# Low parts of two output weights in an attention and convolution kernel: subtracted by GpSimd behind the scaling of the probabilities, or by VectorE behind the row maximum

## The chip, the cores and the metric

The kernel runs on one core of one Trainium2 chip. A core has five engines that run their own instruction rows and wait for each other by semaphores: TensorE (PE in the profile, with its weight loads as PEld), VectorE (DVE), ScalarE (ACT), GpSimd (POOL) and SyncE (SP, which here only issues DMAs). The metric is the device time of one execution in microseconds (us), the median of the runs.

## The reference, cut to what matters

Two layers work on 1024 latent tokens of width 1024, with 256 context tokens. The first is attention with a window of 128 on each side, 16 query heads on 4 key heads, a learned sink in the softmax and a gate; the second is a gated convolution of width 31. Each ends in an output projection with a weight of 2048 x 1024:

```python
p_ctx, p_win = sink_softmax(sink_l, s_ctx, s_win)
o = einsum('bhgqc,bchd->bqhgd', p_ctx, vc) + einsum('bhgqk,bkhd->bqhgd', p_win, vw)
y = (o * silu(z)) @ attn_w_out            # first layer
...
y = (u * silu(z)) @ conv_w_out            # second layer
x = x + gate * y
```

All is float32. The kernel gets near this with TensorE's rounded float32 by splitting each operand into a rounded high part and the rest, the low part, and adding three products: high by high, high by low, low by high.

## The kernel before, in words

Everything is tiled in 128 partitions. SBUF is held as 45 pages of 1024 words (`pg`, line 113) and 6 half pages of 528 words (`hp`, line 114), which go round in a queue: a page that is freed is given out again, and its new writer waits for its last reader.

The program has three stages. First come the norms and modulation of the first layer. Then attention (lines 1083 to 1127) goes through 16 heads of 8 query blocks, 128 steps. Last come the first output projection, the convolution layer and the second output projection. TensorE's row is kept in the order of the program (`pin("P")`, line 1064); the rows of the other engines are set by a scheduler that simulates the kernel, within the dependencies, so that an edit can move instructions which it does not name.

One attention step does this. TensorE computes the scores of the next block into a PSUM tile `pss` (`scores`, line 938). VectorE adds mask and sink and takes the row maximum (`p_page<-pss,mask_page,nsink`, a custom instruction, line 966, with a read of its accumulator into `sc`). ScalarE takes the exponential in place (`p_page,sc<-p_page,sc`, line 968), VectorE the reciprocal of the row sum (`sc<-sc`, line 969), GpSimd scales the probabilities by it (`p_page<-p_page,sc`, line 970). Meanwhile TensorE runs 12 matmuls of the projections of the next head (`psg<-hh_page,whi_page` and the like, `fill(FILL)`, line 1105). Then it transposes the scaled probabilities of the block before (`pss<-ident,p_page`, `transposes`, line 973). ScalarE rounds the transposed block into `pthi`, VectorE subtracts that from it into `ptlo` (lines 991 and 992). Every fourth step TensorE multiplies `pthi` and `ptlo` by the values (`pso<-pthi,kvc_page`, `pv`, line 994). The scores and the transposes share two PSUM tiles, so that the scores of a step wait for the `ptlo` or the maximum that last read the tile.

Beside the steps run these jobs. The weights of the projections are loaded (`wraw_page`), rounded by ScalarE (`whi_page`), and GpSimd subtracts (`wlo_page<-wraw_page,whi_page`, 128 x 1024). The queries of the next head are rotated: ScalarE copies them, a DMA swaps halves, GpSimd multiplies by the sines (`rope_half<-rope_half,sin_page`), VectorE adds, ScalarE rounds (`qh_page`), and GpSimd subtracts (`ql_page<-rope_half,qh_page`). VectorE also sums the modulation of the second layer (`mask_page<-wsum_raw,cs,mask_page` and the same with `dww_raw`, `ada_rest`, line 566).

One more job is `low_parts` (line 613): 32 pieces of the two output weights, two rows of 512 words each, are loaded into a page (`low_page`), ScalarE rounds each half into a half page (`lhi_half`, line 622), the difference replaces the half (`low_page<-low_page,lhi_half`, 128 x 512, line 623), and SP stores the page to DRAM (`wolA<-low_page`, `wolC<-low_page`, line 627), from where the projections read it later. That is 64 subtractions, done by VectorE. The helper `after` (line 561) adds an ordering without a semaphore: VectorE's subtraction stands behind the last row maximum (`anchor_max`).

Of the kernel before, what the change touches and what calls it, by code (L numbers as in the profile page):

```python
# [12 lines left out]
ALU = mybir.AluOpType  # L13
# [80 lines left out]
def backbone_kernel(  # L94
# [8 lines left out]
    V, A, G, PE, SY = (InOrder(tc, e) for e in (nc.vector, nc.scalar, nc.gpsimd, nc.tensor, nc.sync))  # L103
# [18 lines left out]
    def ps_s():  # L122
        return ps.tile([P, 1024], F32, tag="s", name=nm("pss"), bufs=2)
# [21 lines left out]
    def small(shape, dt=F32, name="sm", bufs=2):  # L145
        return cpool.tile(shape, dt, tag=f"{name}", name=nm(name), bufs=bufs)

    def act(out, in_, func, **kw):
        return A.activation(out=out, in_=in_, func=func, **kw)

    def tt(eng, out, a, b, op):
        return eng.tensor_tensor(out=out, in0=a, in1=b, op=op)
# [4 lines left out]
    def split_lo(eng, lo, full, hi):  # L157
        return tt(eng, lo, full, hi.bitcast(F32), ALU.subtract)
# [333 lines left out]
    for pr in range(NPR):  # L492
        a, b = 2 * pr, 2 * pr + 1
# [51 lines left out]
    mask = mask_pg[:, 0:768]  # L545
# [10 lines left out]
               for t, n in (("dww", NJ * TAPS), ("wsum", NJ * 16))]  # L556

    anchor = []
    anchor_max = []

    def after(ins, anchor=anchor):
        if anchor:
            tc.add_manual_dep(ins.ins, anchor[0].ins.name, mybir.DependencyInfo(
                mybir.DependencyClass.NoSync, mybir.DependencyReason.DATA), reason="behind the softmax")
# [44 lines left out]
    def pair_rows(ap, m, kk):  # L609

        return ap[kk * 256:kk * 256 + 256, m * 512:m * 512 + 512].rearrange("(a p) n -> p a n", p=P)

    def low_parts():

        items = [(pair_rows(w, m, kk), d[m, kk]) for w, d in ((Wo, wolA), (Wp, wolC)) for m in range(2) for kk in range(NK)]
        for src, dst in items:
            raw = pg.alloc(F32, [2, 512], "low")
            SY.dma_start(out=raw, in_=src)
            yield "open"
            for b in range(2):  # L620
                hi = hp.alloc(F32R, None, "lhi")
                act(hi[:, 0:512], raw[:, b], AF.Copy)
                after(split_lo(V, raw[:, b], raw[:, b], hi[:, 0:512]), anchor_max)
                hp.free(hi)
                if b == 0:
                    yield "open"
            SY.dma_start(out=dst, in_=raw)
            pg.free(raw)
            yield "shut"
# [308 lines left out]
    def scores(h, qb):  # L938
        g = h // 4
        q = qt[h]  # L940
        kk = kvt[g]
        c = kk[2]
        k0, k1 = max(qb - 1, 0), min(qb + 1, TB - 1)
        nw = (k1 - k0 + 1) * P
        s = ps_s()
        w0 = 512 - nw
        qsl = slice(qb * P, qb * P + P)
        ksl = slice(k0 * P, k0 * P + nw)
        for n, (a, b) in enumerate(((0, 0), (0, 1), (1, 0))):
            PE.matmul(s[:, w0:512], q[a][:, qsl], kk[b][:, ksl], start=n == 0, stop=n == 2)  # L950
            PE.matmul(s[:, 512:768], q[a][:, qsl], c[:, b], start=n == 0, stop=n == 2)
        p = pg.alloc(F32, [1024], "p")
        sc8 = small([P, 3], name="sc", bufs=6)
        nmx, l0, ri = (sc8[:, i:i + 1] for i in range(3))
        w = nw + CT

        act(p[:, w:w + 1], nsink[:, h:h + 1], AF.Copy)
        sc = dict(scale=-SCALE, scalar=nsink[:, h:h + 1], op0=ALU.add, op1=ALU.min, accum_out=nmx)
        if qb == TB - 1:
            least = V.tensor_tensor_reduce(  # L960
                out=p[:, 0:w].rearrange("p (a b) -> p a b", a=2),
                in0=s[:, w0:768].rearrange("p (a b) -> p a b", a=2),
                in1=mask.rearrange("p (a b) -> p a b", a=2)[:, :, 0:256],
                **sc)
        else:
            least = V.tensor_tensor_reduce(out=p[:, 0:w], in0=s[:, w0:768], in1=mask[:, 640 - w:640], **sc)
        anchor_max[:] = [least]
        act(p[:, 0:w + 1], p[:, 0:w + 1], AF.Exp, bias=nmx, scale=-1.0, accum_out=l0)
        V.reciprocal(ri, l0)
        G.tensor_scalar(out=p[:, 0:w], in0=p[:, 0:w], scalar1=ri, scalar2=1.0, op0=ALU.mult, op1=ALU.mult)  # L970
        ptile[(h, qb)] = p

    def transposes(h, qb):
# [73 lines left out]
    for kt in range(KT):  # L1047
        x_mm(kt, 1, acc1, range(3))
        if kt + 2 < KT:
            x_tile(turn(xs1, kt + 2, lambda: ps_o(kt % 2)), kt + 2, 1, G if kt % 2 and kt > 1 else V)  # L1050
        if kt > 2 and ropes0:
            ropes0.popleft()()
        if kt == 3:
            ctx0("v", 2)
        if kt >= 2 and tails:
            tails.pop(0)()
        if kt == 0:
            wsA.load()
        if kt == 5:
            pg.free(*xs1)  # L1060
            wsA.split()
        if kt == KT - 1:
            scores(0, 0)
# [6 lines left out]
    while len(tails) > 1:  # L1070
        tails.pop(0)()
    steps = [(h, qb) for h in range(NH) for qb in range(TB)]
    lows = low_parts()
    lstate = ["shut"]
    pvq = deque()
# [7 lines left out]
    for i, (h, qb) in enumerate(steps):  # L1083
# [18 lines left out]
        if nxt and not regroup:  # L1102
            scores(*nxt)
# [4 lines left out]
        if regroup:  # L1108
            g = nxt[0] // 4
            old = kvt[g - 1]  # L1110
            run(job(("k", g)))
            transposes(h, qb)
            run(job(("v", g)))
            pv(h, 1)
            pg.free(*old)
            scores(*nxt)
            vlate.pop(g)()
            continue
# [576 lines left out]
```

## Time and profile before

| what | value |
|---|---|
| runs of the kernel before | 1777.82, 1778.02, 1778.15 us; median 1778.02 |
| the profiled execution | 1782.36 us, its span 1780.1 us |
| TensorE busy | 1722.9 us, 97% of the span |
| VectorE, ScalarE, GpSimd busy | 1203.3, 885.6, 780.4 us |
| mean granted TensorE clock | 0.991 |
| HBM read and written | 188.70 MB and 41.69 MB |

A row of the timeline gives start, duration, engine, line, operation, what is written from what, shapes and, in brackets, how long the engine idled before it and what released it. All instructions go through one helper (line 88), so they are told apart by the names of their tiles. In the answers by tile, least, median and longest durations are in ns. Times in the windows and the timeline are us from the span's start. The profiled execution is 4.34 us longer than the median of the runs.

### The profile page before, as it was taken

How to read it: one execution, taken by the hardware profiler on the slowest of the kernel's cores; microseconds unless marked ns; L12 is line 12 of the kernel's file. 1: busy time of each engine (PE TensorE's matmuls, PEld its weight loads, DVE VectorE, ACT ScalarE, POOL GpSimd, SP SyncE). 2: the span in 40 equal slices, each digit the busy share in tenths (PEclk: the TensorE clock that was granted, in tenths of full speed). 3: DMA queues.
4: the chain of work that ended last, by engine and by line, in shares of the span. 5: the costliest groups of instructions: out<-in, count | busy, mean ns of one | idle time of the engine just before them, and what ended most of it. 6: DMA issues, size and time to landing. Idle time of an engine off the chain costs nothing. (4 is left out here: it accounts for less than half of the span.)

```text
span 1780.1 us, 23728 instructions
## 1 busy us (share of the span) xinstructions
PE 1722.9 (97%) x8383; PEld 1419.1 (80%) x8383; DVE 1203.3 (68%) x2165; ACT 885.6 (50%) x1540; POOL 780.4 (44%) x610
## 2 busy tenths in 40 slices
PE   5999999999999999999999999999999999999997
PEld 2788888788887888788888887888888888787886
DVE  6766774667555664666314269999999999866823
ACT  6555543455344453444433445654656565456730
POOL 0244343333423343432100247998988789120300
PEclk8999999999999999999999999999999999999999
DMA  9334443444234443336776733111121212377881
GB/s 311 102 81 139 143 127 93 125 147 145 80 116 131 142 150 93 114 100 206 256 248 241 260 94 102 29 48 36 36 83 36 73 46 71 120 245 237 311 281 48
DMA packets 195322, 242.43 MB, mean 136 GB/s; under 512 B 11798, under 2 KB 126790, under 8 KB 195204
## 3 DMA queue, kind: packets, MB, share of 16 engines
q1 hardware_dynamic: 188516, 230.10, 39.8%
q10 hardware_dynamic: 6688, 10.83, 2.6%
q8 instruction: 66, 1.08, 0.3%
q14 instruction: 52, 0.43, 0.1%
HBM read 188.70 MB, written 41.69 MB: 129 GB/s over the span
## 5 line engine op out<-in xcount | busy, mean ns | idle before, releaser
L88 POOL TENSOR_TENSOR odd_half<-odd_half,prod_half 128x513 f32<-128x513 f32 (+2 forms) x252 | 317.9, 1269 | 20.8 <-ACT prod_half L88 7.3
L88 POOL TENSOR_TENSOR wlo_page<-wraw_page,whi_page 128x1024 fp32r<-128x1024 f32 x71 | 173.8, 2449 | 153.0 <-ACT whi_page L88 115.6
L88 POOL TENSOR_SCALAR p_page<-p_page,sc 128x640 f32<-128x640 f32 (+1 forms) x128 | 104.2, 815 | 307.7 <-DVE sc L88 280.2
L88 PE MATMUL psg<-hh_page,whi_page 128*128 128x512 f32 x600 | 237.6, 396 | 0.0
L88 PE MATMUL psg<-hh_page,wlo_page 128*128 128x512 f32 x600 | 236.3, 394 | 0.0
L88 PE MATMUL psg<-hl_page,whi_page 128*128 128x512 f32 x600 | 236.0, 393 | 0.0
L88 ACT ACTIVATE prod_half<-ubuf,dww 128x513 f32<-128x513 f32 (+2 forms) x252 | 165.0, 674 | 108.6 <-POOL odd_half L88 104.4
L88 PE MATMUL psg<-h2l_page,whi_page 128*128 128x512 f32 x456 | 180.6, 396 | 1.8 <-DVE h2l_page L88 1.8
L88 PE MATMUL psg<-h2h_page,whi_page 128*128 128x512 f32 x456 | 181.5, 398 | 0.0
L88 PE MATMUL psg<-h2h_page,wlo_page 128*128 128x512 f32 x456 | 180.1, 395 | 0.0
L88 DVE SCALAR_TENSOR_TENSOR pss<-ubuf,wsum,pss 128x512 f32<-128x512 f32 (+3 forms) x270 | 172.3, 671 | 0.3
L88 DVE SCALAR_TENSOR_TENSOR pss<-ubuf,dww,pss 128x512 f32<-128x512 f32 (+3 forms) x270 | 172.1, 671 | 0.3
L88 ACT ACTIVATE p_page<-p_page,sc 128x641 f32<-128x641 f32 (+1 forms) x128 | 102.9, 804 | 91.8 <-DVE sc L88 87.3
L88 ACT ACTIVATE pthi<-pss 128x640 fp32r<-128x640 f32 (+1 forms) x144 | 88.7, 616 | 104.7 <-PE pss L88 98.0
L88 DVE TENSOR_TENSOR ptlo<-pss,pthi 128x640 fp32r<-128x640 f32 (+1 forms) x144 | 103.1, 716 | 45.7 <-ACT pthi L88 45.3
L88 PEld LDWEIGHTS psg<-hh_page,wlo_page 128*128 128x128 f32 x600 | 112.8, 188 | 26.2
L88 ACT ACTIVATE whi_page<-wraw_page 128x1024 fp32r<-128x1024 f32 x88 | 92.8, 1054 | 73.9 <-PE psg L88 22.3
L88 PEld LDWEIGHTS psg<-hl_page,whi_page 128*128 128x128 f32 x600 | 112.9, 188 | 20.1
L88 PEld LDWEIGHTS psg<-hh_page,whi_page 128*128 128x128 f32 x600 | 112.8, 188 | 20.0
L88 PE MATMUL pso<-h2l_page,whi_page 128*128 128x512 f32 x312 | 122.9, 394 | 0.0
L88 PE MATMUL pso<-h2h_page,wlo_page 128*128 128x512 f32 x312 | 122.8, 393 | 0.0
L88 PE MATMUL pso<-h2h_page,whi_page 128*128 128x512 f32 x312 | 122.7, 393 | 0.0
(240 smaller groups left out, 4026.8 us busy)
## 6 DMA issues: line engine op xcount, KB each, us to landing
wraw_page<-in_conv_w_in_dram SPq DMA_DIRECT2D x48, 512.0 KB
wraw_page<-in_attn_w_in_dram SPq DMA_DIRECT2D x40, 512.0 KB
wo_page<-in_attn_w_out_dram SPq DMA_DIRECT2D x32, 512.0 KB
wol_page<-wolA SPq DMA_DIRECT2D x32, 512.0 KB
wo_page<-in_conv_w_out_dram SPq DMA_DIRECT2D x32, 512.0 KB
wol_page<-wolC SPq DMA_DIRECT2D x32, 512.0 KB
rope_half<-rope_half ACTq DMA_DIRECT2D x80, 128.0 KB
araw_page<-in_ada_w_dram SPq DMA_DIRECT2D x32, 256.0 KB
```

Of the source, the lines that this page charges most:

```text
L88: r = f(*a, **k)
```

## The change

The 64 subtractions go from VectorE to GpSimd, and the instruction behind which they stand is now the last scaling of the probabilities, GpSimd's own, and not the last maximum on VectorE. Nothing else is edited.

```diff
     anchor = []
-    anchor_max = []
+    anchor_p = []
...
-                after(split_lo(V, raw[:, b], raw[:, b], hi[:, 0:512]), anchor_max)
+                after(split_lo(G, raw[:, b], raw[:, b], hi[:, 0:512]), anchor_p)
...
         if qb == TB - 1:
-            least = V.tensor_tensor_reduce(
+            V.tensor_tensor_reduce(
...
         else:
-            least = V.tensor_tensor_reduce(out=p[:, 0:w], in0=s[:, w0:768], in1=mask[:, 640 - w:640], **sc)
-        anchor_max[:] = [least]
+            V.tensor_tensor_reduce(out=p[:, 0:w], in0=s[:, w0:768], in1=mask[:, 640 - w:640], **sc)
         act(p[:, 0:w + 1], p[:, 0:w + 1], AF.Exp, bias=nmx, scale=-1.0, accum_out=l0)
         V.reciprocal(ri, l0)
-        G.tensor_scalar(out=p[:, 0:w], in0=p[:, 0:w], scalar1=ri, scalar2=1.0, op0=ALU.mult, op1=ALU.mult)
+        anchor_p[:] = [G.tensor_scalar(out=p[:, 0:w], in0=p[:, 0:w], scalar1=ri, scalar2=1.0, op0=ALU.mult, op1=ALU.mult)]
```

TensorE's row is the same instruction for instruction. VectorE's has 64 fewer and GpSimd's 64 more. ScalarE's and SP's rows have the same instructions, some of them in another order.

VectorE, in the fifth head, around the 18th low part (at 315.80 us in the trace of before). `p_page` with two results is the row maximum and `sc` alone its accumulator's read, `zs` the gate:

```order
 L88 ISA p_page_2976,sc_2977<-pss_2969,mask_page_699,nsink 128x640
 L88 ISA sc_2977 128x1
-L88 TENSOR_TENSOR low_page_2967<-low_page_2967,lhi_half_3005 128x512
 L88 RECIPROCAL sc_2977<-sc_2977 128x1
 L88 ISA p_page_3015,sc_3016<-pss_3008,mask_page_699,nsink 128x640
 L88 ISA sc_3016 128x1
-L88 TENSOR_TENSOR low_page_2967<-low_page_2967,lhi_half_3072 128x512
 L88 SCALAR_TENSOR_TENSOR zs_page_2852<-zs_page_2852,psg_2944 128x512
 L88 TENSOR_TENSOR ptlo<-pss_2995,pthi 128x5x128
```

Behind each maximum the low part is gone: the reciprocal follows directly in the first step, and `zs` and `ptlo` in the second.

GpSimd, at the end of the fifth head, where `ql_page_3025` is the low part of the next head's queries (at 333.39 us in the trace of before):

```order
 L88 TENSOR_SCALAR p_page_3083<-p_page_3083,sc_3084 128x640
 L88 TENSOR_TENSOR rope_half_3141<-rope_half_3141,sin_page_624 128x512
 L88 TENSOR_SCALAR p_page_3127<-p_page_3127,sc_3128 128x512
+L88 TENSOR_TENSOR low_page_3118<-low_page_3118,lhi_half_3174 128x512
 L88 TENSOR_TENSOR ql_page_3025<-rope_half_3142,qh_page_3024 128x512
 L88 TENSOR_SCALAR p_page_3207<-p_page_3207,sc_3208 128x512
+L88 TENSOR_TENSOR low_page_3118<-low_page_3118,lhi_half_3237 128x512
 L88 TENSOR_TENSOR rope_half_3190<-rope_half_3190,sin_page_624 128x512
 L88 TENSOR_TENSOR wlo_page_3320<-wraw_page_2940,whi_page_3319 128x1024
```

A low part now stands between the scaling and `ql`, and another one step later ahead of the product with the sines and of `wlo`.

ScalarE, in the sixth head, where `lhi_half_3497` is the rounding of a low part (at 349.59 us in the trace of before) and the two `pthi` are the halves of one transposed block:

```order
 L88 ACTIVATE qh_page_3024<-rope_half_3191 128x512
-L88 ACTIVATE zs_page_3214<-psg_3215 128x512
-L88 ACTIVATE lhi_half_3497<-low_page_3436 128x512
 L88 ACTIVATE pthi<-pss_3292 128x2x128
 L88 ACTIVATE p_page_3362<-nsink 128x1
 L88 ACTIVATE pthi<-pss_3292 128x2x128
+L88 ACTIVATE lhi_half_3497<-low_page_3436 128x512
 L88 ACTIVATE p_page_3312,sc_3313<-p_page_3312,sc_3313 128x641
```

The rounding has moved from ahead of both `pthi` to behind them, ahead of the exponential.

## The prediction

> **What bounds the kernel now.** I read the page's head first, then the busy time in three stretches, then TensorE's waits in the middle one, then its pauses one by one in the timeline, and beside each what VectorE, GpSimd and ScalarE did.
>
> ```profile
> span 1780.1 us, 23728 instructions
> PE 1722.9 (97%) x8383; PEld 1419.1 (80%) x8383; DVE 1203.3 (68%) x2165; ACT 885.6 (50%) x1540; POOL 780.4 (44%) x610
> 89.00:890.00 801.00, 778.16 (x4238) 664.40 (x4237) 486.44 (x938) 373.76 (x784) 297.88 (x253) 1.00 0.43 133
> ```
>
> TensorE sets the time: it is busy 97% of the span. The third row is attention (the columns are the stretch, its length, then PE, PEld, DVE, ACT and POOL busy, the clock, the DMA share and GB/s): 801.00 − 778.16 = 22.8 us are pauses of TensorE. No change to the other engines can gain more there, and it gains only by ending pauses. Who ends them, in that stretch (total us, times, longest):
>
> ```profile
> PE pss L88 <- DVE ptlo L88: 5.6, 8, 1.1
> PE pso L88 <- DVE ptlo L88: 3.5, 7, 1.1
> PE pss L88 <- POOL p_page L88: 1.5, 4, 0.5
> ```
>
> 9.1 us wait for `ptlo`, the low halves of the transposed probabilities. Seven of those pauses, from the timeline of TensorE (the bracket is the pause before the matmul):
>
> ```profile
> 318.99 0.50 PE L88 MATMUL pso<-ptlo,kvc_page 128*128 128x512 f32 x1 [1.14 <-DVE ptlo L88]
> 383.27 0.44 PE L88 MATMUL pss<-kh_page,qh_page 128*128 128x384 f32 x1 [1.09 <-DVE ptlo L88]
> 404.72 0.44 PE L88 MATMUL pss<-kh_page,qh_page 128*128 128x384 f32 x1 [1.00 <-DVE ptlo L88]
> 521.09 0.50 PE L88 MATMUL pso<-ptlo,kvc_page 128*128 128x512 f32 x1 [1.14 <-DVE ptlo L88]
> 586.14 0.44 PE L88 MATMUL pss<-kh_page,qh_page 128*128 128x384 f32 x1 [0.91 <-DVE ptlo L88]
> 607.73 0.44 PE L88 MATMUL pss<-kh_page,qh_page 128*128 128x384 f32 x1 [0.83 <-DVE ptlo L88]
> 755.23 0.44 PE L88 MATMUL pss<-kh_page,qh_page 128*128 128x384 f32 x1 [0.59 <-DVE ptlo L88]
> ```
>
> What made `ptlo` late before the first, on VectorE, and what GpSimd ran meanwhile:
>
> ```profile
> 315.80 1.80 DVE L88 TENSOR_TENSOR low_page<-low_page,lhi_half 128x512 f32<-128x512 f32 x1
> 317.53 0.67 DVE L88 SCALAR_TENSOR_TENSOR zs_page<-zs_page,psg 128x512 f32<-128x512 f32 x1
> 318.13 0.81 DVE L88 TENSOR_TENSOR ptlo<-pss,pthi 128x640 fp32r<-128x640 f32 x1
> ```
> ```profile
> 314.63 2.43 POOL L88 TENSOR_TENSOR wlo_page<-wraw_page,whi_page 128x1024 fp32r<-128x1024 f32 x1
> ```
>
> The subtraction of a low part (`low_page`) reads two SBUF operands and ends at 317.60, 0.54 us after GpSimd's `wlo` at 317.06: it does not run beside it but behind it. `ptlo`, queued behind, has one operand in PSUM and keeps its usual length. The other six pauses have the same pair in front of them, with low parts of 1.82 us (the shortest) to 2.67 (the longest). Over all 64 the group's first row, by the tile, has least, median and longest, its second, by the line, the busy time and the mean:
>
> ```profile
> 517.88 1.82 DVE L88 TENSOR_TENSOR low_page<-low_page,lhi_half 128x512 f32<-128x512 f32 x1
> 752.18 2.67 DVE L88 TENSOR_TENSOR low_page<-low_page,lhi_half 128x512 f32<-128x512 f32 x1
> L88 DVE TENSOR_TENSOR low_page<-low_page,lhi_half x64: 680/687/2860, 149.5 to 777.5; 128x512 f32<-128x512 f32 x64
> L88 DVE TENSOR_TENSOR low_page<-low_page,lhi_half 128x512 f32<-128x512 f32 x64 | 60.9, 951 | 0.0
> ```
>
> The median is 687 ns, the mean 951: 64 × 0.264 = 16.9 us of VectorE are this blocking. The busy shares alone would have hidden it: VectorE is busy 486.44 of 801 us there, far from full, and yet it is late at these places, because one instruction stands behind another engine's.
>
> **The change part by part.** *The seven pauses.* VectorE loses the 60.9 us. At the first place `zs` could start at 315.80 in place of 317.53, so `ptlo` is done 1.73 earlier, and the pause was 1.14. The order after the change puts nothing with two SBUF operands between the row maximum and `ptlo` at any of the seven places, and a blocked low part is longer than the pause at each, so all go: 1.14 + 1.09 + 1.00 + 1.14 + 0.91 + 0.83 + 0.59 = **6.7 us gained**. Next late there would be the high half, `pthi` on ScalarE, which ended at 316.06, well before the blocked subtraction did (317.60), so nothing takes the place of the wait:
>
> ```profile
> 315.36 0.70 ACT L88 ACTIVATE pthi<-pss 128x640 fp32r<-128x640 f32 x1
> ```
>
> *The four pauses on `p_page`.* These transposes wait for a scaling on GpSimd, and in the order before the change a low part stands between the maximum and the reciprocal that this scaling needs. VectorE's reciprocal comes at least 0.6 us sooner without it, the pauses are 0.5 at most: **1.5 us gained**. The ends are 0, if the exponential on ScalarE is what the reciprocal waits for, and 1.5.
>
> *ScalarE's row.* Two pauses come from a rounding `lhi` that waits in line for its page, with `pthi` behind it:
>
> ```profile
> 349.59 0.63 ACT L88 ACTIVATE lhi_half<-low_page 128x512 fp32r<-128x512 f32 x1 [2.80 <-DMA low_page<-in_attn_w_out_dram]
> 552.15 0.63 ACT L88 ACTIVATE lhi_half<-low_page 128x512 fp32r<-128x512 f32 x1 [2.44 <-DMA low_page<-in_conv_w_out_dram]
> 351.90 0.74 PE L88 MATMUL pss<-ident,p_page 128*128 128x128 f32 x5 [1.31 <-DVE sc L88]
> 554.45 0.74 PE L88 MATMUL pss<-ident,p_page 128*128 128x128 f32 x5 [0.94 <-DVE sc L88]
> ```
>
> In the first place `pthi` starts only at 350.13, and the row maximum that TensorE waits for stands behind its `ptlo`. The new order puts that `lhi` behind both `pthi` in the first place, and behind the first of the two in the second. Then `ptlo` and the maximum are no longer late: 1.31 + 0.94 = 2.25, **2.2 us gained**; none, if the loads or the exponential now behind them become the last.
>
> *What GpSimd takes on.* No low part on GpSimd is in the trace. The nearest row is the same subtraction for `ql`, 128x512:
>
> ```profile
> L88 POOL TENSOR_TENSOR ql_page<-rope_half,qh_page x28: 1272/1308/1550, 133.7 to 787.7; 128x512 fp32r<-128x512 f32 x28
> L88 POOL TENSOR_SCALAR p_page<-p_page,sc 128x640 f32<-128x640 f32 (+1 forms) x128 | 104.2, 815 | 307.7 <-DVE sc L88 280.2
> ```
>
> 64 × 1.308 = 83.7 us. The ends are 1.27 (its shortest) and 1.55 (its longest); I take the median. GpSimd idles 307.7 us before its 128 scalings, 2.4 us each, so most low parts fit into idle time, and the roundings they wait for are done earlier on ScalarE. Queued behind them are the next scaling, `wlo`, the rope product and `ql`. The first two have spare time; `ql` has none at the start of heads 5, 9 and 13, where the scores follow it at once, and there the new order puts a low part right in front of it:
>
> ```profile
> 333.39 1.55 POOL L88 TENSOR_TENSOR ql_page<-rope_half,qh_page 128x512 fp32r<-128x512 f32 x1 [0.19 <-ACT qh_page L88]
> 535.75 1.52 POOL L88 TENSOR_TENSOR ql_page<-rope_half,qh_page 128x512 fp32r<-128x512 f32 x1 [0.27 <-ACT qh_page L88]
> 737.86 1.27 POOL L88 TENSOR_TENSOR ql_page<-rope_half,qh_page 128x512 fp32r<-128x512 f32 x1 [0.84 <-ACT qh_page L88]
> PE pss L88 <- POOL ql_page L88: 0.9, 2, 0.6
> ```
>
> (The scores' own waits for it come to 0.9 us now.) Of 1.308 us the idle time in front hides 0.19, 0.27 and 0.84: 1.12 + 1.04 + 0.47 = **2.6 us lost**; less, if the scaling before it starts sooner.
>
> *Buffers and queues.* Pages and half pages of a low part come free later, SP stores them later and so issues the loads behind them later, and GpSimd's 64 new reads can block VectorE's other two-operand instructions. Nothing shows the price; the ends are 0 and the rivals below. I take **1.5 us lost**, near the low end, because every wait of that kind that I follow below has been moved in the order.
>
> *The sum.* −6.7 − 1.5 − 2.2 + 2.6 + 1.5 = −6.3. The profiled execution took 1782.36 (span 1780.1 and 2.26 around it), 4.34 above the median of the runs; it would take 1776.1, and the runs 1778.02 − 6.3 = **1771.7 us**.
>
> **The rivals.** *One lock for another (no change).* The low part now locks out what VectorE still does with two SBUF operands, mostly the sums of the second modulation:
>
> ```profile
> L88 DVE SCALAR_TENSOR_TENSOR mask_page<-wsum_raw,cs,mask_page 128x256 f32<-128x256 f32 x64 | 41.1, 643 | 1.9 <-DMA wsum_raw<-in_ada_w_dram 1.7
> L88 DVE SCALAR_TENSOR_TENSOR mask_page<-dww_raw,cs,mask_page 128x256 f32<-128x256 f32 x48 | 33.3, 693 | 0.7 <-DMA dww_raw<-in_ada_w_dram 0.7
> 774.67 2.07 DVE L88 SCALAR_TENSOR_TENSOR mask_page<-wsum_raw,cs,mask_page 128x256 f32<-128x256 f32 x1
> 777.60 0.39 PE L88 MATMUL pss<-kh_page,qh_page 128*128 128x256 f32 x1 [1.10 <-DVE sc L88]
> ```
>
> The last two rows show such a sum, stretched to 2.07, ending in a pause of 1.10. The 83.7 us are 13% of the 640 us in which low parts run, so some 14 of the 112 sums would meet one. If half of these cost 1.10, the gain is eaten: 1771.7 + 7.7 = 1779.4. Against it: a low part blocks for 1.3 us at most where `wlo` blocks for 2.4, and the sums mostly stand behind `ptlo`. The Trainium skill (Perfetto Trace Analysis, "Optimizing Scalar/DVE Operations") speaks for it: GpSimd and VectorE share an SBUF read port, so moving operations from one to the other might not help. By that rule the sum would be this rival's 1779.4, by the rows of the seven pauses it is 1771.7.
>
> *Pages held too long (slower).* ScalarE writes into pages that a low part's store must leave first:
>
> ```profile
>   ACT p_page L88: 23.2, 14
>   ACT whi_page L88: 8.8, 4
> 362.90 1.06 ACT L88 ACTIVATE whi_page<-wraw_page 128x1024 fp32r<-128x1024 f32 x1 [2.92 <-DMA wolA<-low_page]
> 365.46 0.50 PE L88 MATMUL pso<-ptlo,kvc_page 128*128 128x512 f32 x1 [0.18 <-DVE ptlo L88]
> ```
>
> 18 waits, 32.0 us, 1.78 each. What stands behind such a write on ScalarE is a `pthi` or an exponential. A wait of 2.92 reached TensorE as a pause of 0.18, so about 2.7 are covered. The store leaves later by at least the scaling and the longer subtraction, 0.815 + 1.308 − 0.951 = 1.2 us, and by more where the scaling is late. At twice that, 2.4, each wait is 4.2 and 1.5 of it uncovered: 18 × 1.5 = 27 us, 1799. It turns the gain into a loss that can be measured once 7 of the 18 pass on (7 × 1.5 = 10.5, 1782.2). Against it: in the new order every one of the 18 writes stands at least one activation later than before.
>
> **How the numbers follow.** The sum's own case, all or most of it, gets 0.65; the lock 0.21; the pages 0.14. A measurement of this kernel can tell 0.2%, 3.6 us, from no change: faster is below 1774.5, slower above 1781.6. Faster 0.65, same 0.21, slower 0.14. The low end is the sum without the two losses, with 2.6 us more from shorter pauses of VectorE that I left in: 1778.0 − 10.4 − 2.6 = 1765. The high end takes in the lock, 1779.4, and leaves out the pages: 1780.
>
> **What would show it.** Right: no `low_page` on VectorE, the seven pauses gone, TensorE's wait for `ptlo` under 3 us, low parts near 1.31 us on GpSimd, waits for `ql` up from 0.9 to some 3 us. The lock: sums of `mask_page` with a mean above 0.75 us and pauses behind them. The pages: ScalarE's `p_page` waiting for `wolA` and `wolC` well above 23 us, with `pthi` late. I am wrong if TensorE's pauses in attention do not fall from 22.8 to about 16.

## The result, and the profile after

The changed kernel takes 1768.22 us (median; 1766.66 to 1769.78), the kernel before 1778.09 beside it: a ratio of 0.9941 (95% interval 0.9927 to 0.9955). It is 9.9 us faster; the forecast was 6.3 us, 1771.7 in a range of 1765 to 1780. Measured again beside the experiments it came to 1769.62 against 1781.96, a ratio of 0.993 (0.9918 to 0.9943).

The head of the page after, and the stretch that holds the same work as 89 to 890 us before (it begins 0.9 and ends 12.2 us earlier; columns as there):

```profile
span 1767.3 us, 23750 instructions
PE 1718.6 (97%) x8383; PEld 1419.1 (80%) x8383; DVE 1164.4 (66%) x2101; ACT 887.0 (50%) x1540; POOL 859.6 (49%) x674
88.10:877.80 789.70, 774.78 (x4237) 665.29 (x4237) 447.19 (x874) 375.30 (x784) 376.21 (x317) 0.99 0.44 135
```

The stretch is 11.3 us shorter. Pauses fell from 22.8 to 789.70 − 774.78 = 14.9, 7.9 less, and TensorE's busy time in it by 3.4 for the same matmuls, which is new. What it still waits for there, in part:

```profile
PE pss L88 <- DVE sc L88: 3.6, 4, 1.9
PE pss L88 <- POOL ql_page L88: 3.0, 3, 1.1
PE pss L88 <- DVE ptlo L88: 3.0, 4, 1.2
PE pso L88 <- DVE ptlo L88: 0.2, 1, 0.2
```

`ptlo` fell from 9.1 to 3.2 (the prediction's sign was under 3), `p_page` is gone from the list, `ql` rose from 0.9 to 3.0. The first of the seven places, in the timelines of VectorE, GpSimd and TensorE:

```profile
314.12 0.68 DVE L88 SCALAR_TENSOR_TENSOR zs_page<-zs_page,psg 128x512 f32<-128x512 f32 x1
314.72 0.82 DVE L88 TENSOR_TENSOR ptlo<-pss,pthi 128x640 fp32r<-128x640 f32 x1
315.45 1.69 DVE L88 SCALAR_TENSOR_TENSOR mask_page<-wsum_raw,cs,mask_page 128x256 f32<-128x256 f32 x1
```
```profile
313.20 1.29 POOL L88 TENSOR_TENSOR low_page<-low_page,lhi_half 128x512 f32<-128x512 f32 x1
314.46 2.40 POOL L88 TENSOR_TENSOR wlo_page<-wraw_page,whi_page 128x1024 fp32r<-128x1024 f32 x1
```
```profile
315.77 0.39 PE L88 MATMUL pso<-pthi,kvc_page 128*128 128x512 f32 x1
316.00 0.39 PE L88 MATMUL pso<-ptlo,kvc_page 128*128 128x512 f32 x1
```

`zs` and `ptlo` keep their usual 0.68 and 0.82 us beside GpSimd's operations, and TensorE has no pause. The operation that now stands still behind `wlo` is the modulation sum after `ptlo`, 1.69 us, for which nobody waits.

Since executions differ by a few us outside attention, I compare kernels below also by the time from the first transposes to the last, read from TensorE's timeline like these two rows of the kernel after (746.8 us; before it was 869.28 − 111.28 = 758.0). The profile of the kernel before is of an execution 4.3 us above its median, so a distance to it can come out too large; the ratios of the runs do not have this fault.

```profile
110.42 0.60 PE L88 MATMUL pss<-ident,p_page 128*128 128x128 f32 x4
857.22 0.60 PE L88 MATMUL pss<-ident,p_page 128*128 128x128 f32 x4
```

One thing differs from profile to profile in that time, and the table below lists it: stretches of 3.4 or 6.8 us in which the granted clock of TensorE is 0.50 (1.00 is full speed). The kernel after has two (the clock is the third number from the right):

```profile
725.10:728.50 3.40, 2.97 (x8) 2.49 (x9) 1.52 (x4) 1.58 (x5) 1.66 (x2) 0.50 0.17 41
834.30:841.10 6.80, 6.19 (x19) 5.12 (x20) 4.92 (x8) 6.19 (x10) 2.05 (x3) 0.50 1.05 406
```

In the first of them the matmuls of the projections start every 0.43 us in place of 0.23, so a stretch of 3.4 us costs some 1.6 us (an estimate from these two distances). The 14 profiles have 26 such stretches in attention. Each begins in a pause of TensorE or within 1.0 us of its end, with at least 1.6 us of pauses in the 4 us before it; but not every such sum of pauses is followed by one, and what decides it is not shown.

### The profile page after: what moved, and what is told of

Its sections match the earlier page's. It is cut to its first block, busy times and chain, and to the rows that moved or that the text cites. A ratio compares the mean times of both kernels' runs of the same rounds, so it can differ in the third digit from the quotient of the medians.

```text
span 1767.3 us, 23750 instructions
## 1 busy us (share of the span) xinstructions
PE 1718.6 (97%) x8383; PEld 1419.1 (80%) x8383; DVE 1164.4 (66%) x2101; ACT 887.0 (50%) x1540; POOL 859.6 (49%) x674
## 3 DMA queue, kind: packets, MB, share of 16 engines
q8 instruction: 66, 1.08, 0.3%
## 5 line engine op out<-in xcount | busy, mean ns | idle before, releaser
L88 ACT ACTIVATE whi_page<-wraw_page 128x1024 fp32r<-128x1024 f32 x88 | 92.8, 1054 | 66.6 <-PE psg L88 22.8
```

The costliest lines, as they stand in the source:

```text
L88: r = f(*a, **k)
```

## The experiments

The theory (A in the expectations) is that of the prediction: a VectorE operation on two SBUF operands waits for a running GpSimd operation, and what is queued behind it makes TensorE pause. The main rival is the place: the low part stood in front of `ptlo`, and any place behind it would do. The kernel before ran beside every group. "Attention" is first to last transposes, in one profile of each, and "half clock" the part of it with a granted clock of 0.50.

The trace of the kernel before speaks for the lock already, over all 64 low parts. 20 of them took over 0.8 us. Each of these began while a GpSimd operation ran (10 times `wlo`, 7 times `ql`, twice a scaling, once the product with the sines), and each ended 0.53 to 0.56 us after it. Of the other 44, all of them short, one began beside a GpSimd operation, a scaling.

| kernel | time, us | ratio to before (95%) | attention, us | half clock, us |
|---|---|---|---|---|
| before | 1778.09 | | 758.0 | 6.8 |
| the change | 1768.22 | 0.9941 (0.9927 to 0.9955) | 746.8 | 10.2 |
| VectorE, behind `ptlo` | 1771.72 | 0.9948 (0.9933 to 0.9963) | 752.2 | 13.7 |
| GpSimd, behind the maximum | 1772.53 | 0.9962 (0.9950 to 0.9973) | 748.5 | 3.4 |
| no subtraction | 1770.71 | 0.9952 (0.9934 to 0.9970) | 749.0 | 6.8 |
| before, `wlo` in halves | 1770.49 | 0.9943 (0.9926 to 0.9959) | 750.0 | 10.2 |
| the change again | 1769.62 | 0.9930 (0.9918 to 0.9943) | 746.7 | 3.4 |
| low part behind `ql` | 1765.31 | 0.9914 (0.9900 to 0.9928) | 743.7 | 3.4 |
| early load | 1786.44 | 1.0027 (1.0018 to 1.0036) | 767.6 | 34.1 |
| the change, `wlo` in halves | 1764.16 | 0.9904 (0.9891 to 0.9918) | 744.0 | 10.2 |
| VectorE, behind `ptlo`, halves | 1768.45 | 0.9929 (0.9916 to 0.9942) | 747.0 | 10.2 |
| behind `ql`, and halves | 1762.69 | 0.9895 (0.9880 to 0.9909) | 740.2 | 6.8 |
| the same, early load | 1768.66 | 0.9932 (0.9919 to 0.9945) | 745.2 | 6.8 |
| low part twice | 1771.22 | 0.9938 (0.9924 to 0.9951) | 745.0 | 6.8 |

The kernels below the change were measured in three groups, beside medians of 1780.23, 1781.96 and 1780.93 of the kernel before, so times of different groups are compared by their ratios. A difference of 1 or 2 us in attention between two profiles can be a stretch at half clock alone.

**The length of the lock.** The kernel before, with GpSimd's operation cut in two:

```diff
-                split_lo(self.lo_eng(i), l, r, h)
+                n = KT // 2 if i > 3 else KT
+                for k in range(0, KT, n):
+                    ks = slice(k, k + n)
+                    split_lo(self.lo_eng(i), l[:, ks], r[:, ks], h[:, ks])
```

> The kernel before, with each wlo of the attention stage subtracted in two pieces of 128x512 on GpSimd in place of one of 128x1024. All other rows stand as before. Theory A (the lock lasts as long as the one running operation of GpSimd): a low part is blocked for 1.3 us at most, so its longest falls from 2.86 to about 2.0 and its mean from 0.95 to about 0.85, the seven pauses (0.59 to 1.14) mostly go, and the time falls by 4 to 7 us, to 1771 to 1774. If VectorE cannot get in between the two pieces, nothing changes, and the lock lasts as long as GpSimd has work. Rival D (the low parts were late for another reason, their page or the rounding): mean 0.95 and 1778 us, within 1.

Measured: 1770.49 us, attention 8.0 us shorter, with the low parts still on VectorE and in front of `ptlo`. The groups of `wlo` and of the low part, then the latter's durations, then TensorE's waits for `ptlo`:

```profile
L88 POOL TENSOR_TENSOR wlo_page<-wraw_page,whi_page 128x512 fp32r<-128x512 f32 x72 | 100.5, 1417 | 55.5 <-ACT whi_page L88 32.9 <-DVE oz_half L88 11.5 <-ACT p_page L88 5.8
L88 DVE TENSOR_TENSOR low_page<-low_page,lhi_half 128x512 f32<-128x512 f32 x64 | 52.3, 817 | 0.2 <-ACT lhi_half L88 0.2
```
```profile
L88 DVE TENSOR_TENSOR low_page<-low_page,lhi_half x64: 680/689/1803, 149.8 to 768.4; 128x512 f32<-128x512 f32 x64
```
```profile
PE pss L88 <- DVE ptlo L88: 1.8, 4, 0.5
PE pso L88 <- DVE ptlo L88: 1.8, 5, 1.0
```

The longest low part falls from 2.86 to 1.80 us, all seven pauses are gone, and so is the one of 1.10 on `sc` at 777.60; GpSimd itself works 12 us longer in attention. VectorE gets in between the two pieces, as at the longest low part:

```profile
200.96 1.80 DVE L88 TENSOR_TENSOR low_page<-low_page,lhi_half 128x512 f32<-128x512 f32 x1
200.90 3.04 POOL L88 TENSOR_TENSOR wlo_page<-wraw_page,whi_page 128x512 fp32r<-128x512 f32 x2 [3.35 <-ACT whi_page L88]
```

The first piece took 1.32 us, the low part ended 0.55 after it, and the second piece, beside it, took 1.77 in place of the usual 1.30: VectorE holds GpSimd up in turn. This shows the mechanism: almost nothing but the length of one GpSimd operation was changed (one row of VectorE's and one of ScalarE's changed places).

**The place.** The low part on VectorE, behind the last `ptlo`:

```diff
-                after(split_lo(V, raw[:, b], raw[:, b], hi[:, 0:512]), anchor_max)
+                after(split_lo(V, raw[:, b], raw[:, b], hi[:, 0:512]), anchor)
```

> The subtractions stay on VectorE, but stand behind the last ptlo in place of the last row maximum. Theory A (the engine: a low part on VectorE stands still behind a running operation of GpSimd, wherever it is put): its mean stays near 0.95 us, its longest over 2 us, the seven pauses go, and others come up where the row maximum or the reciprocal stands behind it; TensorE's pauses in attention stay above 17 us (before 22.6, after the change 14.9) and the time comes to 1772 to 1777 us. Rival B (the place: a low part in front of ptlo was the fault, and VectorE had room for it): pauses near 15 us and the changed kernel's time, 1768 us, within 2.

Measured: in between. Attention gains 5.8 us of the change's 11.2 (with some 3.4 us more at half clock than after the change). The low part's mean falls to 0.78 and its longest to 1.78, where theory A had 0.95 and over 2; all seven pauses are gone here too, and others come at the row maximum:

```profile
L88 DVE TENSOR_TENSOR low_page<-low_page,lhi_half 128x512 f32<-128x512 f32 x64 | 49.6, 776 | 0.0
```
```profile
PE pss L88 <- DVE sc L88: 8.7, 5, 2.8
PE pss L88 <- DVE ptlo L88: 1.7, 3, 1.3
```

The waits for `ptlo` fall, as the place theory has it; those for `sc` rise from 5.7 to 8.7, as the theory of the lock has it. Two of the five, of 1.08 (new) and 2.77 us (1.10 before), stand behind a low part that a GpSimd operation stretched to 1.78 and 1.75; two others, of 1.56 and 1.36, stand behind a rounding that waits for its load, as before. Both cures together, still on VectorE:

> The low parts on VectorE behind the last ptlo (as in the first experiment), and each wlo of the attention stage on GpSimd in two pieces. Theory A (both cures act on the same lock: one takes the low parts out of its way, the other makes it short): attention falls from the 752.2 us of the first experiment, from the first transposes to the last, to 746 to 749, and with no move to GpSimd the time comes within 2 us of the changed kernel's 1768 to 1770. Rival B2 (VectorE has no room for the 64 low parts, its load itself makes it late): attention stays above 750.5 us, 1771 us or more.

Measured: attention 747.0, 1768.45 us, the changed kernel's own, although the waits for `sc` are still 7.5. So VectorE had room for the 64 low parts, and the move to GpSimd was not needed for this gain: it is one of several ways out of the lock.

**The other order on GpSimd.** The changed kernel with `anchor_max` in place of `anchor_p`, so that a low part may stand in front of a scaling:

> The subtractions run on GpSimd as in the change, but ordered behind the row maximum as before, which lets GpSimd take some of them ahead of a scaling. Theory A (the engine): no low part on VectorE, so the seven pauses are gone; a scaling with a low part in front of it is up to 1.3 us later, which its spare time (the scaling is ready 2 us or more ahead of its transposes nearly everywhere) takes in: 1766 to 1771 us. Rival B (the place): the order behind the scaling is what brings the gain, so a low part ahead of the scaling delays the transposes: TensorE's waits for p_page of over 5 us (before 1.5, after the change none above 0.2) and 1775 us or more.

Measured: 1772.53 us, 1.5 above the theory's range, attention 1.7 us longer than after the change. TensorE waits 0.4 us for `p_page`, not over 5, so the rival's sign did not come. The evidence from this run is thin, since only five scalings were held up by a low part, by 0.5 to 1.5 us; the run with the low part twice, below, had 22 held up by 0.5 to 3.4 us, and there too TensorE had no wait of over 0.15 us for `p_page`. So a scaling that comes this much later does not delay the transposes. The place behind the scaling is worth little; the rows of ScalarE and VectorE differ too, which the run does not separate.

**GpSimd's share, taken away and doubled.** The line with the subtraction is left out in one kernel, and stands twice in the other:

> The 64 subtractions are left out altogether (what is stored is the whole weight, not its low part). Theory A (the sum of the prediction): what GpSimd took on costs the late ql, 2.0 to 2.6 us, and 1 to 1.5 for pages, queues and the lock on VectorE's sums: the waits for ql fall from 3.0 to 1 us or less, the mean of the sums of mask_page from wsum_raw from 0.81 to about 0.65, and the time is 1764 to 1766 us. Rival C (GpSimd's share costs nothing, what pauses remain have other causes): 1768 us, within 1.5.

> The change with every low part subtracted twice on GpSimd one behind the other (the second subtraction takes the rounded part off again, so that what is stored is no longer the low part): 64 more operations of 1.3 us. Theory A (GpSimd has room, and only what stands right behind a low part pays): ql waits 3 x 1.3 us more, VectorE's two-operand sums are blocked more often, together 4 to 7 us slower than the changed kernel. Rival E (stores that leave 1.3 us later hold pages and stall ScalarE): its waits for wolA and wolC rise from 11.8 us to over 30 and the time by over 10 us. Theory C (GpSimd's share is free): within 1.5 us of the changed kernel.

Measured: without the subtraction 1770.71, not 1764 to 1766, and also above rival C's 1768 with its 1.5; twice 1771.22. (The profile of the latter, with attention at 745.0, is of the fastest run, 1765.14; the other five took 1770.95 to 1771.59, so its attention is not that of the median.) TensorE's waits without it, and, in the second fence, with it twice:

```profile
PE pso L88 <- DVE ptlo L88: 2.7, 3, 2.0
PE pss L88 <- DVE ptlo L88: 2.7, 5, 1.0
PE pss L88 <- POOL ql_page L88: 1.0, 2, 0.5
```
```profile
PE pss L88 <- POOL ql_page L88: 5.4, 3, 2.9
```

The waits for `ql` fell to 1.0 as expected and rose to 5.4, by 2.4 where 3.9 was expected. ScalarE's waits for the stores rose from 11.8 to 21.6 with the subtraction twice, not over 30, so rival E's sign did not come. But waits for `ptlo` went the other way, 5.4 and 1.3 against 3.2, because an edit also moves ScalarE's and VectorE's rows. By the ratios, 0.9952 and 0.9938 beside 0.9941 and 0.9930, rival C stands in the total: 83 us more of GpSimd's work cost nothing that can be measured, and 83 us less gained nothing. These two runs cannot price a single term, since ScalarE's row alone shows some 130 lines of difference to the changed kernel's in the first.

**The late `ql`.** A cut that leaves the other rows nearly alone, at the ends of heads 4, 8 and 12 only:

```diff
+        first = nxt and nxt[1] == 0 and nxt[0] % 4 == 1
+        due = lstate[0] == "open" or h and (h % 4 < 3 or qb < LOWS)
+        if due and not first:
+            lstate[0] = next(lows, "shut")
         if nxt and nxt[1] == 0:
             fill(1000, ("q", h + 1))
+        if due and first:
+            anchor_p[:] = last_q
+            lstate[0] = next(lows, "shut")
```

> The change, and at the ends of heads 4, 8 and 12 alone the low part in front of the first ql of the next head is put behind ql; elsewhere the rows stay as in the changed kernel. Theory A (the low part makes ql late, as the prediction's loss of 2.6 us had it): TensorE's waits for ql fall from 3.0 us to about 0.9, and the time is 2.0 to 2.6 us under that of the changed kernel in the same call. Rival C (ql is late by its own operands, or its lateness is taken over by the next wait): waits for ql above 2 us or a time within 1 us of the changed kernel's.

> The changed kernel itself once more, beside the three others: what its time is on this chip, how far its runs spread, and whether the pauses of its first profile (ql 3.0 us, ptlo 3.2, sc 3.6, 14.8 us in all) come back at the same places. Theory A (pauses set by the rows): the same places within 0.3 us each, 13.5 to 16.5 us in all, ratio to before 0.9930 to 0.9955. Rival (pauses are chance): other places, 3 us or more away in sum.

Measured: 1765.31 beside 1769.62 (the intervals of their ratios overlap), attention 3.0 us shorter. The waits for `ql` are 1.7, not 0.9; a pause of 1.2 on `ptlo` at 544 us, which the change had brought, went too:

```profile
PE pss L88 <- POOL ql_page L88: 1.7, 3, 0.8
```

(The load that the rounding in front of it had waited for came in time here; why was not tried.) So the direction of A holds, and the 3.0 us are part `ql` and part this load. The change's own second profile has `ql` at 3.3 and attention at 746.7, 0.1 from the first. That this agrees so well is luck: the second has 2.8 us more pauses and 6.8 us less at half clock, by the estimate above 3.2 us. Single pauses move (one of 0.82 on `sc` and one of 0.88 on `rope_half` were not there the first time), and all pauses came to 17.7, out of the range that I gave. A single pause below 1 us in one profile is not yet a property of the rows.

**The rest of the lock.** `wlo` in halves in the changed kernel:

> The change, with each wlo of the attention stage in two pieces of 128x512. Theory A (what is left of the lock after the change falls on VectorE's modulation sums and rope additions, and decides little): the pause of 1.10 on sc at 764 us goes, the mean of the sums from wsum_raw falls from 0.81 to about 0.75, the time falls by 1 to 2 us. Theory F (halving wlo and moving the low parts are two cures of one fault and the second adds nothing): within 1 us of the changed kernel. Rival G (12 us more work on a GpSimd that now has less spare time): the scaling becomes late, waits for p_page over 2 us, slower by 2 us or more.

Measured: 1764.16, 5.5 us less than the change beside it, with attention 2.7 us shorter in a profile of its slowest run: more than A's 1 to 2 either way, and against F and G. The pause of 1.10 on `sc` is gone, and those on `rope_half` fell from 2.3 us in the second profile of the change to 0.2: VectorE's addition of the rotated queries also has two SBUF operands. Both cures together:

> The change with both cures that gained by themselves: at the ends of heads 4, 8 and 12 the low part behind ql, and wlo in two pieces. Theory A (they end different pauses, so the gains add but for the pause on ptlo behind a waiting rounding, which both ended): attention 741 to 743 us (746.7 after the change, 743.7 and 744.0 with one of them), time 5 to 8 us under the changed kernel's, a ratio of 0.988 to 0.990 to before. Theory F (they are the same gain twice): 743.5 to 744.5 and the ratio of either alone.

Measured: 1762.69 us, ratio 0.9895, attention 740.2: the gains add, a little more than fully. This version beats both kernels: 18.2 us under the kernel before beside it, and by its ratio 0.35% under the change, with intervals that do not meet.

**Early loads.** The pause at 544 us came from a rounding that waited for its load with `pthi` behind it:

```profile
542.87 0.63 ACT L88 ACTIVATE lhi_half<-low_page 128x512 fp32r<-128x512 f32 x1 [1.55 <-DMA low_page<-in_conv_w_out_dram]
543.41 0.37 ACT L88 ACTIVATE pthi<-pss 128x256 fp32r<-128x256 f32 x1
544.29 0.45 PE L88 MATMUL pss<-kh_page,qh_page 128*128 128x384 f32 x1 [1.19 <-DVE ptlo L88]
```

So the load went one step ahead:

```diff
             pg.free(raw)
+            if k + 1 < len(items):
+                nraw = load(items[k + 1][0])
             yield "shut"
```

> The change, with each piece of the output weights loaded one step earlier, so that the rounding lhi does not stand at the head of ScalarE's row waiting for its load (40.9 us in 19 waits after the change). Theory A (two of the pauses left after the change, 1.19 and 0.78 on ptlo, come from pthi queued behind such a rounding): lhi's waits for the load under 15 us, those two pauses gone, 2 to 3 us faster than the changed kernel. Rival E (the page that is held a step longer is missed elsewhere): ScalarE's p_page and whi_page wait longer for wolA, wolC or the scaling, and nothing is gained, or up to 5 us lost.

> As the run with both cures, and the loads of the output weights one step earlier, but not across the breaks before a new group of heads, where holding a page early had cost some 15 us. Theory A (the loss was in the rows at the three starts of a group, the early load itself gains): lhi's waits for its load fall from some 40 us to under 20, no pause over 1.5 us on vf or qh at the starts of heads 4, 8 and 12, attention 1 to 3 us shorter than with both cures. Rival E (a page held one step longer delays others wherever it is): attention 2 us or more longer.

Measured: the waits for the load fell, to 6.2 and 12.7 us, and the pauses behind them went, but the kernel became 16.8 us slower, and with the break guarded 6.0 slower than the best version (its attention by 5.0). The first two rows are of the guarded kernel, the third is of the best version at the same place, and the last is the guarded kernel's product with the sines:

```profile
331.12 0.63 ACT L88 ACTIVATE lhi_half<-low_page 128x512 fp32r<-128x512 f32 x1 [3.76 <-DMA rope_half<-rope_half]
334.01 0.39 PE L88 MATMUL pss<-kh_page,qh_page 128*128 128x256 f32 x1 [1.95 <-ACT qh_page L88]
```
```profile
327.70 0.63 ACT L88 ACTIVATE lhi_half<-low_page 128x512 fp32r<-128x512 f32 x1 [1.55 <-DMA rope_half<-rope_half]
331.19 1.29 POOL L88 TENSOR_TENSOR rope_half<-rope_half,sin_page 128x512 f32<-128x512 f32 x1 [5.04 <-DMA rope_half<-rope_half]
```

The rounding waits 3.76 us for its half page, whose last reader is the DMA of the rotation, and the exponential and the reciprocal stand behind it. In the best version the rounding has the same neighbours in ScalarE's row and waits for the same DMA, but only 1.55 us. So the place in the row is not what differs; the DMA is late, and the product with the sines, which `qh` needs too, waits for it as well. Two things go with that. ScalarE issued it 1.05 us later, after 2.64 us of waiting for the store `wolA` in place of 1.58. And the early load (512 KB) was issued between its two halves, at 325.74, where the best version issues its load at 328.89, after the last packet of the rotation. The rotation's packets took 1.9 us in the best version and 3.8 in the guarded kernel, and the queue of the loads moved this in that time (its packets, MB and share of the 16 DMA engines; the best version first):

```profile
q1 hardware_dynamic: 15, 0.02, 3.7%
q1 hardware_dynamic: 396, 0.64, 58.6%
```

That the load is what delayed the rotation is argued from these rows; no run keeps it out of the rotation's way. Rival E had the outcome, and the store in part, but did not name the two DMAs that meet. Theory A was right on where most of the loss was: without the guard attention is 20.8 us longer than after the change, with it 5.0 longer than in the best version, and the pauses on `vf` at the three starts of a group (10.0 us) are gone. It was wrong that the early load then gains.

Much of the unguarded loss is not in the pauses themselves: they grew by 11.2 us, and its 34.1 us at half clock, against 10.2 and 3.4 in the two profiles of the change, account for some 11 to 14 of the 20.8 by the estimate above (the two overlap a little). The largest new pause there follows an addition of the rotation that a `wlo` stretched from 0.69 to 2.81:

```profile
280.00 2.81 DVE L88 TENSOR_TENSOR rope_half<-rope_half,rope_half 128x512 f32<-128x512 f32 x1 [3.98 <-POOL rope_half L88]
284.31 0.69 PE L88 MATMUL pso<-ident,vf_half 128*128 128x128 f32 x2 [5.26 <-ACT vf_half L88]
```

After the change the same addition is held just as long, and TensorE has no pause:

```profile
278.74 0.39 ACT L88 ACTIVATE vf_half<-psg 128x256 f32<-128x256 f32 x1 [1.42 <-PE psg L88]
278.94 2.88 DVE L88 TENSOR_TENSOR rope_half<-rope_half,rope_half 128x512 f32<-128x512 f32 x1 [0.89 <-POOL rope_half L88]
```

There `vf` stands in ScalarE's row ahead of the rounding `kh`, which needs the addition; in the unguarded kernel it stands behind `kh` and a rounding of a low part. So here it is the order of ScalarE's row that makes the lock cost something.

## Why the prediction was right, term by term

TensorE's instructions are the same in both kernels, so the starts of equal matmuls can be laid side by side; where the distance between the two traces jumps, a term shows. From the first transposes to the last it grows by 11.2 us. (The two profiled executions are 13.3 us apart, the medians 9.9, so the terms are those of this pair.)

| term | forecast | in the traces |
|---|---|---|
| the seven pauses | −6.7 | 1.31 + 1.34 + 1.23 + 1.29 + 1.16 + 0.98 + 0.83 = −8.1 |
| four pauses on `p_page` | −1.5 | 0.63 + 0.39 + 0.50 + 0.55 = −2.1 |
| two roundings in ScalarE's row | −2.2 | 1.48 + 1.09 = −2.6 |
| late `ql` at heads 5, 9, 13 | +2.6 | 1.16 + 0.84 + 0.40 = +2.4 |
| pages, queues, lock | +1.5 | five new pauses: 0.38 + 1.06 + 1.03 + 0.24 + 0.88 = +3.6 |
| eight pauses under 0.5 us, not counted | 0 | 0.49 + 0.34 + 0.31 + 0.56 + 0.62 + 0.50 + 0.54 + 0.31 = −3.7 |
| sum | −6.3 | −10.5 (the other 0.7 is the balance of jumps under 0.4) |

*The seven pauses* all went, and were mis-sized: they lasted 6.70, and ending them brought 8.14. Each is worth 0.14 to 0.25 more than its bracket. Before, the matmul after the first of them took 0.50 us and the next started 0.34 later:

```profile
319.33 0.63 PE L88 MATMUL pso<-pthi,kvc_page 128*128 128x512 f32 x2
```

After the change the same matmul takes 0.39, and one starts every 0.23. Matmuls in a row overlap, and a pause breaks the overlap. Matmul by matmul, nearly all of the 3.4 us that fell out of the busy time lies within three matmuls of a pause. The forecast took the bracket as the price.

*The pauses on `p_page`* went in full; the end of 0 that I gave for them did not come. *ScalarE's row*: both pauses went, but at the second place the pause came back as the 1.06, on the next tile, because the rounding still stands ahead of the second `pthi`, as the order had shown.

*`ql`* is late where and by about what was forecast:

```profile
333.09 0.39 PE L88 MATMUL pss<-kh_page,ql_page 128*128 128x256 f32 x1 [1.11 <-POOL ql_page L88]
527.55 0.39 PE L88 MATMUL pss<-kh_page,ql_page 128*128 128x256 f32 x1 [1.12 <-POOL ql_page L88]
725.53 0.58 PE L88 MATMUL pss<-kh_page,ql_page 128*128 128x256 f32 x1 [0.78 <-POOL ql_page L88]
```

The last of the three cost more than its 0.40 in the table: at 725.10, in this pause, the first stretch at half clock begins, and the matmuls that it slows lose another 1.1 us, which the jumps under 0.4 hold. The second profile of the change has the same pause of 0.78 and no such stretch there. The prediction had no term for the clock.

The low part's price on GpSimd, 1.308 by the nearest row, was right:

```profile
L88 POOL TENSOR_TENSOR low_page<-low_page,lhi_half x64: 1268/1294/1479, 151.0 to 766.4; 128x512 f32<-128x512 f32 x64
```

*What was left open at 1.5* came to 3.6, in part by the mechanism that was named: two of the five (1.06 and 1.03) are `pthi` behind a rounding that waits for its load. The 0.88 is `pthi` behind another rounding on ScalarE (`ozh`) that waits for a DMA. In front of none of the five stands a stretched VectorE operation, so the lock, which this term held too, cost nothing here. *The small pauses* brought 3.7; their brackets sum to 2.5, which I had only let into the low end of the range. These two errors, +2.1 and −3.7, cancel in part, by luck. With the overlap of the seven (−1.4), the pauses on `p_page` (−0.6), ScalarE's row (−0.4), `ql` (−0.2) and the small jumps (−0.7) the traces come to 4.9 us more than the forecast's 6.3, and the medians to 3.6 more. So the path was right, the places were right, and the gain was undershot.

*The rival of the lock*: its sign in the profile came, its price did not.

```profile
L88 DVE SCALAR_TENSOR_TENSOR mask_page<-wsum_raw,cs,mask_page 128x256 f32<-128x256 f32 x63 | 51.2, 813 | 0.4 <-DMA wsum_raw<-in_ada_w_dram 0.3
L88 DVE SCALAR_TENSOR_TENSOR mask_page<-dww_raw,cs,mask_page 128x256 f32<-128x256 f32 x48 | 34.8, 725 | 0.5 <-DMA dww_raw<-in_ada_w_dram 0.5
```

The sums grew from 0.645 and 0.693 to 0.813 and 0.725, 63 × 0.168 + 48 × 0.032 = 12.1 us of VectorE. They stand behind `ptlo`, and the one pause of 1.10 that a sum caused was there before. By the Trainium skill (Perfetto Trace Analysis, "Optimizing Scalar/DVE Operations") the shared read port might make such a move useless. The traces agree that the two engines hold each other up (the 20 low parts that ended 0.53 to 0.56 us after a GpSimd operation), but the move gained 9.9 us, since most of the work that is now blocked is work that nobody waits for.

*The rival of the pages* went the other way. ScalarE's waits for the store of a low part fell from 32.0 to 11.8:

```profile
  ACT p_page L88: 10.1, 10
  ACT whi_page L88: 1.7, 3
```

Its step "each wait grows by 1.2" left out what the prediction itself named against it: every such write had been moved to a later place in the row. That this is the whole cause was not tried.

## What to carry to other kernels

When VectorE is far from full and yet late, compare least, median and longest of its two-operand operations, and look what GpSimd ran at the longest; then ask who is queued behind the blocked one. The cures are to shorten GpSimd's operation (here by cutting it in two, for 12 us more of its own time and 8 us less of attention), or to see to it that only operations that nobody waits for are blocked. Where a scheduler sets the rows, price an edit by the pauses that it ends at known places, and expect it to bring others of the same size. When comparing single profiles, look at the granted clock in short windows first.

## What the runs showed that was not expected

A pause of TensorE costs 0.14 to 0.25 us more than it lasts (seven places, 6.70 and 8.14 us). VectorE gets its turn between two GpSimd operations that follow each other: with `wlo` in pieces of 1.30 us (the median) a low part was held at most to 1.80 us, where it had been 2.86. And the granted clock of TensorE fell to 0.50 for 3.4 or 6.8 us behind some pauses of together 1.6 us or more. Two profiles of one kernel agreed to 0.1 us over 747 us of attention only because more pauses in one stood against more time at half clock in the other; single pauses in them differed by up to 1.2 us.
